# An attention's query blocks in another order, and three tiles fewer a head

## The chip, the cores and the metric

One core of a Trainium2 chip runs the whole program. Its engines are TensorE (PE, the matrix products), VectorE (DVE), ScalarE (ACT), GpSimd (POOL) and SyncE (SP); each takes its instructions in the order in which they were written, and waits for others by semaphores. POOL and SP here mostly issue DMA transfers. The metric is the device time of one execution in microseconds (us); of several executions the median counts.

## The reference

Two layers over 1024 rows of 1024 features. The change lies in the attention of the first: eight heads, each with two components of width 64 and values of width 128. A row sees all columns up to the end of its chunk of 64.

```python
def one_block(args):                       # 128 query rows at a time
    s = jnp.einsum('bqhcd,bkhcd->bhcqk', qb, k).astype(jnp.float32)
    s = jnp.where(allowed[None, None, None], s, -jnp.inf)
    p = jax.nn.softmax(s, axis=-1)
    a = p[:, :, 0] - lam * p[:, :, 1]
    return jnp.einsum('bqhk,bkhe->bqhe', a.astype(v.dtype), v)
...
o = rmsnorm(o, subln_g, SUBLN_EPS) * (1.0 - lambda_init)
return o.reshape(B, S, H * ATTN_V_DIM) @ w_o
```

q and k are first turned by rotary factors (`rope`). Around it stand norms, the residual, an MLP, a recurrent layer and a second MLP, which the change doesn't touch.

## The kernel before

**Slots.** The attention runs as 64 slots, eight for each of eight heads. A slot's position in its head picks a block of 128 query rows by the table `ORDER`; block b has scores of (b+1)*128 columns, so block 0 is the shortest and block 7 the longest. All engines but SP run in the order in which the loop of `attention` writes their instructions. What a slot writes, in order:

- `scores` of its block: products on PE (L737, L738), each component as two products with operands that are split in a high and a low part and stacked (`qs`, `ks`); then on DVE a mask and a maximum (L748 and L749 for blocks 0 to 3, whose two components share one bank of PSUM; L757 and L758 for each component of the longer ones), and on ACT the first component's exponential (L741). There are two banks for scores.
- fill work on PE, first part: steps (L584, L585, L587) of the next head's q and k projections, later of the output projection. `FILL_PART` says how much of a head's fill each of the slot's three parts gets.
- `keys_first`: the transposes (L784) of the block of the slot before, and their copies into `aT` on ACT (L961); then the second exponential of the slot's own block.
- one step of the side queue (`run_aside`), and what is due of `later`.
- fill, second part; `weighted`, the products with the values (L794) of the block two slots back, with an eviction and a square on ACT (L795, L797); fill, third part.
- `combine` on DVE (L769, L771, L772) of the slot's own block, and another step of the side queue.

**The side queue** is first in, first out; each of its two calls in a slot hands out one step that is due. Its steps are: the rotary factors of the next head's q or k (L677, L678, L674), each behind the transfers that swap halves; the low part of the product (L688, `low`), after which POOL issues the stacking transfers (L697, L698; four for q, eight for k: component 0 and 1 of one stack, then of the other); the scaling of a half head's output by its norm (L803 in `subln`); the low part of a turned half (L823 in `parts`), after which SP stores it. The high part of a product (L685) runs on ACT as soon as L674 has been written.

**Tiles.** Nearly every tile of 4 KB a partition comes from one pool, T, with 46 places (`BUFS`); they are given out in turn, and whoever writes into a place waits for the last reader of what was there, transfers included.

**Halves.** A head's eight output blocks are gathered as two halves (blocks 0 to 3, 4 to 7) in tiles `o4`. A half is normed and turned (`subln`, `turn_out`: PE L813, ACT L819 and L820) some slots after its block 3 or 7 is weighted; with the order of before, block 7 stands at position 3 and block 3 at position 7.

Functions and tables with the lines of the profile:

Of the kernel before, what the change touches and what calls it, by code (L numbers as in the profile page):

```python
# [9 lines left out]
F32 = mybir.dt.float32  # L10
F32R = mybir.dt.float32r
# [4 lines left out]
P = 128  # L16
# [25 lines left out]
class Second:  # L42
# [19 lines left out]
    def load(self, s):  # L62
        if s < self.loaded or s >= len(self.slots):
            return
        self.loaded = s + 1
        kind, (i, j) = self.slots[s]
        last, wv, hid, get, t4 = self.last, self.wv, self.k.hid, self.nc.sync.dma_start, self.k.t4
        w, x = t4("w2", F32, (P, 2, CH), "R"), t4("h2", F32, (P, 2, CH), "W")
        side = None
        if kind == "P":  # L70
            get(out=w, in_=wv[:, 0, i : i + 2, 0])
        elif kind == "A":
            get(out=w, in_=wv[:, 0, i])
            side = t4("w3", F32, (P, CH))
            get(out=side, in_=wv[:, 1, i, 1])
        elif kind == "B":
            get(out=w[:, 0], in_=wv[:, 1, i, 1 if last else 0])
            side = t4("w3", F32, (P, 2, CH))
            if last:
                get(out=side[:, 0], in_=wv[:, 0, i, 1])  # L80
            else:
                get(out=side, in_=wv[:, 0, i])
        else:
            get(out=w, in_=wv[:, 1, i : i + 2, 0 if kind == "C" or last else 1])
        if kind in "AB":
            at = {"A": 1, "B": 3}[kind]
            get(out=x, in_=hid[i][:, at : at + 2])
        else:
            at = {"P": 0, "C": 5, "D": 6}[kind]
            for n, b in enumerate((i, j)):  # L90
                get(out=x[:, n], in_=hid[b][:, at])
        self.raws[s] = w, x, side
# [158 lines left out]
    def run(self):  # L251
# [11 lines left out]
        self.prepare(0)  # L263
        for s in range(N - TAIL_SLOTS):
            self.load(s + AHEAD)
# [12 lines left out]
            self.drain(budget[kind])  # L278
        tail = range(N - TAIL_SLOTS, N)
        for s in tail[1:]:  # L280
# [10 lines left out]
class Trunk:  # L291
# [389 lines left out]
    def parts_of(self, q, then):  # L681

        nc = self.nc
        h, l = self.t4("qkh", F32R), self.t4("qkl", F32R)
        nc.scalar.activation(out=h, in_=q, func=AF.Copy)  # L685

        def low():
            nc.vector.tensor_tensor(out=l, in0=q, in1=h.bitcast(F32), op=ALU.subtract)  # L688
            then(h, l)

        self.aside(RL, low)
# [137 lines left out]
    def later(self, us, fn):  # L829
# [5 lines left out]
        while us > 0:  # L835
            us -= 2.8 + 0.65 * ORDER[s % NT]
            s += 1
        self.tasks.setdefault(s, []).append(fn)

    def aside(self, us, fn):  # L840
# [5 lines left out]
        while us > 0:  # L846
            us -= 2.8 + 0.65 * ORDER[s % NT]
            s += 1
# [19 lines left out]
    def attention(self):  # L868

        nc = self.nc
        while self.held:
            self.held.pop(0)()
        self.queue = []
        o = [None] * H
        wo = self.ins["attn_w_o"][0]
        blocks = [(h, kind) for h in range(H) for kind in "qk"]  # L880

        def halves(h):
            parts = []
            for p in range(2):
                t = self.t4("o", F32R)
                nc.sync.dma_start(out=t.bitcast(F32), in_=self.oT[h][p])
                parts.append(t)
            return parts

        def ahead(steps, at, box, load):  # L890
            for n, step in enumerate(steps):
                if n == at:
                    box.append(load())
                yield step

        def fills():
            box = [self.w_proj(*blocks[2])]
            first = []
            for b in range(2, len(blocks)):
                load = (lambda: self.w_proj(*blocks[b + 1])) if b + 1 < len(blocks) else (lambda: self.w_out(wo, 0, 4, 0))  # L900
                if b in OLOAD:
                    first += [halves(h) for h in OLOAD[b]]
                yield from ahead(self.proj_steps(*blocks[b], box.pop(0), "G"), 5, box, load)
            self.x = []
            for m in range(NK):
                at = 3 if m % 2 == 1 and m < NK - 1 else -1
                wt = box[0] if m % 2 == 0 else box.pop(0)
                was = self.raw(self.xT[m * P : (m + 1) * P, :], (P, S))
                self.x.append(self.t4("x"))
                yield from ahead(self.out_block(first, wt, m, m % 2, False, None, "G"), at, box, lambda: self.w_out(wo, 0, 4, (m + 1) * P))  # L910
                y = self.x[m]
                self.aside(1, lambda y=y, was=was: nc.vector.tensor_tensor(out=y, in0=y, in1=was, op=ALU.add))

        fill = fills()
        done = 0

        def fill_to(n):
            nonlocal done
            while done < n:
                step = next(fill, None)  # L920
                if step is None:
                    break
                done += step

        rate = (FILL_TOTAL - FILL_LEAD - FILL_KEEP) / H
        self.slot, self.tasks = 0, {}
        fill_to(FILL_LEAD)
        work = {}
        LT, LW, LO = LAGS
        os = []  # L930
        s = -1
        with self.tc.manual_schedule(engines={EPE, EACT, EDVE, EPOOL}):
            while s + 1 < H * NT or work or self.tasks or self.queue:
                s += 1
                self.slot = s
                h, pos = divmod(s, NT)
                i = ORDER[pos]

                def run(part):
                    f = (sum(map(sum, FILL_PART[:pos])) + sum(FILL_PART[pos][:part])) / sum(map(sum, FILL_PART))  # L940
                    if h < H:
                        fill_to(FILL_LEAD + rate * (h + f))
                    else:
                        fill_to(FILL_TOTAL - FILL_KEEP + FILL_KEEP * (3 * pos + part) / (3 * LO))

                os += [halves(g) for g in LATE.get(s - (H - 1) * NT, ())]
                exp2 = None
                if h < H:
                    if pos == 0:
                        if h == H - 1:  # L950
                            o[h] = [self.t4("oh", F32R), self.t4("ol", F32R)]
                        o4 = [self.t4("o4", F32, (P, 4, P)) for _ in range(2)]
                        ss = [self.sm("oss", 4) for _ in range(2)]
                    p, sums, exp2 = self.scores(h, i)
                    work[s] = [h, i, p, sums, o4[i // 4], ss[i // 4]]
                run(1)
                if s - LT in work:
                    wk = work[s - LT]
                    wk[2], outs = self.keys_first(wk[1], wk[2])
                    for dst, src in outs:  # L960
                        nc.scalar.activation(out=dst, in_=src, func=AF.Copy)  # L961
                if exp2:
                    exp2()
                self.run_aside(ASIDE[0])
                for fn in self.tasks.pop(s, ()):
                    fn()
                assert s not in self.tasks
                run(2)
                if s - LW in work:
                    wk = work.pop(s - LW)  # L970
                    self.weighted(*wk)
                    if wk[1] % 4 == 3:
                        self.later(1, lambda wk=wk: self.subln(wk[4], wk[5], lambda: self.turn_out(wk[0], wk[1] // 4, wk[4], o[wk[0]])))
                run(3)
                if s in work:
                    wk = work[s]
                    wk[2], wk[3] = self.combine(wk[1], wk[2], wk[3])
                self.run_aside(ASIDE[1] if h < H else 4)
            for _ in fill:
                pass  # L980
            self.run_aside(len(self.queue))
            self.slot = None
        self.os = os + [halves(h) for h in range(4 + len(os), H - 1)] + [o[H - 1]]
        self.w_lo = None
# [478 lines left out]
RS, RL, RN, RT, R3 = (10, 2, 3, 2, 3)  # L1463
ASIDE = (1, 1)
LAGS = (1, 2, 4)
FILL_PART = [(1.24, 1.17, 0.33), (0.74, 1.39, 0.4), (0.52, 1.0, 0.14), (0.74, 1.26, 0.4), (0.74, 1.0, 0.56), (0.79, 0.94, 0.37), (0.89, 1.18, 0.4), (1.04, 1.23, 0.4)]
ORDER = (4, 5, 6, 7, 0, 1, 2, 3)
ROWS = ((slice(0, HD), slice(HD, P)), (slice(HD, P), slice(0, HD)))
EPE, EACT, EDVE, EPOOL, ESP = (getattr(mybir.EngineType, e) for e in ("PE", "Activation", "DVE", "Pool", "SP"))
FILL_TOTAL, FILL_LEAD, FILL_KEEP = (288, 30, 10)  # L1470
OLOAD = {13: (0,), 14: (1, 2), 15: (3,)}
ORDER_A = (0, 1, 4, 5, 2, 3, 6, 7)
LATE = {7: (4,)}
TAIL_SLOTS = 4
AHEAD = 4
BUFS = {"R": 4, "W": 4, "T": 46}
# [26 lines left out]
```

## Time and profile before

| what | value |
|---|---|
| median of 3 executions | 2273.68 us (2269.03 to 2278.88) |
| the profiled execution | 2282.74 us, its span 2280.9 us |
| mean granted clock of TensorE in it | 0.975 |
| busy share of the span | PE 94%, DVE 67%, ACT 47%, POOL 4% |
| attention (158 to 610 us of the span) | 452 us, PE busy 383.67 us, clock 0.94 |

Times in the trace are microseconds from the span's start. The granted clock is a share of full speed: the clock has two levels, 1.0 (2.4 GHz) and 0.5 (1.2 GHz), and a share between them is a mean over a stretch. A row `[2.64 <-DVE p L772]` says that the engine sat idle 2.64 us before the instruction, and what ended the wait last by the profile.

### The profile page before, as it was taken

Reading aid. Unit: us, or ns where it says so; the run is one execution under the profiler, and the core shown is the slowest. Engines: PE = TensorE matmul, PEld = TensorE weight load, DVE = VectorE, ACT = ScalarE, POOL = GpSimd, SP = SyncE. Lnnn points to the kernel's source line nnn. Section 1 sums busy time; section 2 is a strip of 40 time slices with the busy share of each in tenths; the row PEclk is TensorE's granted clock in tenths of the full one; section 3 lists DMA queues with packets and bytes.
Section 4 is the critical chain, followed back from the end, with each engine's and each line's share of the span. In section 5 each row is a group of like instructions: output and inputs, shape, how many; then the busy total and the mean of one; then the engine's idle time right before and its main releaser. Section 6 shows DMA issues by size and latency. Waiting matters only on the chain.

```text
span 2280.9 us, 26452 instructions
## 1 busy us (share of the span) xinstructions
PE 2143.6 (94%) x9794; PEld 1763.2 (77%) x9794; DVE 1526.2 (67%) x2065; ACT 1069.0 (47%) x1627; POOL 102.6 (4%) x171
## 2 busy tenths in 40 slices
PE   8998888887999999999999999988999999799997
PEld 7786777776788888878888787777788888688885
DVE  5426667655697777658778467775977776476665
ACT  5225555554564444444335356652644443353433
POOL 3111112111000000000000000000000000000000
PEclk9999999988999999999999999998999999899999
DMA  6534435634524444398556412234244444874734
GB/s 193 143 83 114 114 102 133 167 106 113 178 97 153 152 153 152 136 371 282 208 178 219 133 46 85 72 111 143 102 156 152 152 152 150 323 254 162 239 111 147
DMA packets 236227, 355.82 MB, mean 156 GB/s; under 512 B 16226, under 2 KB 133059, under 8 KB 236099
## 3 DMA queue, kind: packets, MB, share of 16 engines
q1 hardware_dynamic: 227266, 326.87, 42.9%
q0 software_dynamic: 7680, 25.17, 4.8%
q10 hardware_dynamic: 1152, 2.10, 0.3%
q8 instruction: 77, 1.26, 0.2%
q14 instruction: 52, 0.42, 0.1%
HBM read 229.29 MB, written 91.23 MB: 141 GB/s over the span
## 4 chain that ended last, share of the span: by engine, by line
PE 62%; DVE 11%; ACT 10%; DMA 5%; issue 4%; POOL 1%; SPq 0%; ACTq 0%; POOLq 0%; DVEq 0%
PE acc L1192 5%; PE acc L1193 5%; PE acc L1194 5%; PE acc L145 4%; PE acc L143 4%; PE acc L144 4%; PE acg L1192 2%; PE acg L1194 2%; PE acg L1193 2%; ACT p L741 2%; PE acg L584 2%; PE acg L585 2%; PE acg L587 2%; PE acc L584 2%; PE acb L144 2%
## 5 line engine op out<-in xcount | busy, mean ns | idle before, releaser
L341 DVE TENSOR_TENSOR h2l<-h,h2h 128x1024 fp32r<-128x1024 f32 x112 | 136.7, 1221 | 72.5 <-ACT h2h L338 68.8
L1095 ACT ACTIVATE ct<-ct 128x1024 f32<-128x1024 f32 x64 | 67.9, 1061 | 250.3 <-DVE ct L1164 249.3
L741 ACT ACTIVATE p<-acc,nmax 128x768 f32<-128x768 f32 (+7 forms) x128 | 95.4, 745 | 153.3 <-DVE nmax L758 56.9
L338 ACT ACTIVATE h2h<-h 128x1024 fp32r<-128x1024 f32 x112 | 117.5, 1049 | 59.4 <-DMA h<-hid 51.4
L584 PE MATMUL acg<-xgh,wh 128*128 128x512 f32 x320 | 135.7, 424 | 0.0
L587 PE MATMUL acg<-xgh,wl 128*128 128x512 f32 x320 | 127.9, 400 | 0.0
L585 PE MATMUL acg<-xgl,wh 128*128 128x512 f32 x320 | 127.7, 399 | 0.0
L338 ACT ACTIVATE w2h<-w 128x1024 fp32r<-128x1024 f32 x80 | 84.2, 1053 | 86.1 <-DVE w L56 70.5
L143 PE MATMUL acc<-w2h,h2h 128*128 128x512 f32 x256 | 102.9, 402 | 7.2 <-ACT w2h L338 5.6
L144 PE MATMUL acc<-w2l,h2h 128*128 128x512 f32 x256 | 102.6, 401 | 5.4 <-DVE w2l L341 5.4
L414 POOL TENSOR_TENSOR rstd<-ms,mhalf 128x4 f32<-128x4 f32 (+2 forms) x25 | 25.0, 1002 | 1798.5 <-DVE ms L412 1777.9
L143 PE MATMUL acc<-h2h,w2h 128*128 128x512 f32 x256 | 101.1, 395 | 4.4 <-ACT w2h L338 4.2
L145 PE MATMUL acc<-h2h,w2l 128*128 128x512 f32 x256 | 101.5, 396 | 3.6 <-DVE w2l L341 3.6
L1164 DVE TENSOR_TENSOR cl<-cl,acc 128x512 f32<-128x512 f32 x64 | 60.9, 951 | 64.6 <-PE acc L1194 64.6
L341 DVE TENSOR_TENSOR w2l<-w,w2h 128x1024 fp32r<-128x1024 f32 x80 | 97.8, 1222 | 8.9 <-PE acc L144 4.9
L1192 PE MATMUL acc<-t12h,w12h 128*128 128x512 f32 x256 | 100.5, 393 | 2.4 <-DVE ct L1164 2.4
L145 PE MATMUL acc<-w2h,h2l 128*128 128x512 f32 x256 | 102.1, 399 | 0.0
L144 PE MATMUL acc<-h2l,w2h 128*128 128x512 f32 x256 | 101.2, 395 | 0.4 <-DVE h2l L341 0.4
L1193 PE MATMUL acc<-t12l,w12h 128*128 128x512 f32 x256 | 100.3, 392 | 0.0
L1194 PE MATMUL acc<-t12h,w12l 128*128 128x512 f32 x256 | 100.2, 391 | 0.0
L794 PEld LDWEIGHTS acb<-v,aT 128*128 128x128 f32 x576 | 74.8, 198 | 28.9 <-ACT aT L961 23.9
L794 PE MATMUL acb<-v,aT 128*128 128x128 f32 x576 | 80.1, 286 | 13.2 <-ACT aT L961 12.5
(377 smaller groups left out, 6077.4 us busy)
## 6 DMA issues: line engine op xcount, KB each, us to landing
w<-in_mlp_w_dram SPq DMA_DIRECT2D x96, 512.0 KB, 4.9
raw<-in_mlp_w_dram SPq DMA_DIRECT2D x64, 512.0 KB, 4.5
h<-hid SPq DMA_DIRECT2D x64, 512.0 KB, 5.3
h<-hid SPq DMA_DIRECT2D x96, 256.0 KB, 5.3
w<-in_mlp_w_dram SPq DMA_DIRECT2D x80, 256.0 KB, 4.0
hid<-cl SPq DMA_DIRECT2D x64, 256.0 KB, 2.0
hid<-h SPq DMA_DIRECT2D x32, 512.0 KB, 2.6
hid<-h SPq DMA_DIRECT2D x64, 256.0 KB, 2.1
```

Source lines behind the costliest of these rows:

```text
L143: mm(bank[m], ah, bh, start=first, stop=False)
L144: mm(bank[m], ah, bl, start=False, stop=False)
L145: mm(bank[m], al, bh, start=False, stop=end)
L338: nc.scalar.activation(out=hi, in_=src, func=AF.Copy)
L341: (lo_eng or nc.vector).tensor_tensor(out=lo, in0=src, in1=hi.bitcast(F32), op=ALU.subtract)
L584: mm(ps[:, pc], a, xh[:, cs], start=(k == 0), stop=False)
L585: mm(ps[:, pc], a, xl[:, cs], start=False, stop=False)
L587: mm(ps[:, pc], b, xh[:, cs], start=False, stop=(k == n - 1))
L794: nc.tensor.matmul(ps[:, :P], aT[:, j * P : (j + 1) * P], v[j // 2][:, j % 2, e], start=(j == 0), stop=(j == i))
L1192: mm(bank, ah[:, k], bh, start=k == 0, stop=False)
L1193: mm(bank, ah[:, k], bl, start=False, stop=False)
L1194: mm(bank, al[:, k], bh, start=False, stop=k == 3)
```

## The change

It has four parts. `ORDER` becomes (7, 0, 6, 1, 5, 2, 4, 3); `FILL_PART` is permuted with it, so that each block keeps its three numbers. The low part of a product is written over the product itself rather than into a tile `qkl`. The two `o4` tiles of a head become the halves of one. And a half is normed after the block of it that comes last in `ORDER` (`LAST_OF`: block 4, at position 6, and block 3, at position 7), since with the new order blocks 3 and 7 no longer end both halves.

```diff
@@ parts_of
-        h, l = self.t4("qkh", F32R), self.t4("qkl", F32R)
+        h, l = self.t4("qkh", F32R), q.bitcast(F32R)
@@ attention
-                        o4 = [self.t4("o4", F32, (P, 4, P)) for _ in range(2)]
+                        both = self.t4("o4", F32, (P, 2, 4, P))
+                        o4 = [both[:, 0], both[:, 1]]
...
-                    if wk[1] % 4 == 3:
+                    if wk[1] in LAST_OF:
@@ tables
-FILL_PART = [(1.24, 1.17, 0.33), (0.74, 1.39, 0.4), (0.52, 1.0, 0.14), (0.74, 1.26, 0.4), (0.74, 1.0, 0.56), (0.79, 0.94, 0.37), (0.89, 1.18, 0.4), (1.04, 1.23, 0.4)]
-ORDER = (4, 5, 6, 7, 0, 1, 2, 3)
+FILL_PART = [(0.74, 1.26, 0.4), (0.74, 1.0, 0.56), (0.52, 1.0, 0.14), (0.79, 0.94, 0.37), (0.74, 1.39, 0.4), (0.89, 1.18, 0.4), (1.24, 1.17, 0.33), (1.04, 1.23, 0.4)]
+ORDER = (7, 0, 6, 1, 5, 2, 4, 3)
...
+LAST_OF = [max((i for i in ORDER if i // 4 == g), key=ORDER.index) for g in range(2)]
```

Behind the tables' change the instructions of a head stand in another order. Two places show it. In the listings a row is a line, an operation, what it writes and what it reads; a number behind a name is the tile's.

VectorE in head 2, where the low part of head 3's k is made (the tile k, its high part `qkh`). Before, at position 4 (block 0, 128 columns):

```order
L748 MEMSET acc_2527 64x2x64
L749 TENSOR_REDUCE nmax<-acc_2527 128x2
L803 TENSOR_TENSOR o_240_1744<-o_240_1744,rstd 128x512
L769 RECIPROCAL rsum<-sums 128x2
L771 SCALAR_TENSOR_TENSOR fac<-sums,rsum,neglam 128x1
L772 SCALAR_TENSOR_TENSOR p_2525<-p_2526,fac,p_2525 128x128
L688 TENSOR_TENSOR qkl_2494<-k_2073,qkh_2493 128x1024
```

After, at position 6 (block 4, 640 columns), from the step ahead of it:

```order
L823 TENSOR_TENSOR ohl_2508<-ot_2507,ohl_2508 128x512
L757 MEMSET acc_2612 64x64
L758 TENSOR_REDUCE nmax<-acc_2612 128x1
L757 MEMSET acc_2619 64x64
L758 TENSOR_REDUCE nmax<-acc_2619 128x1
L823 TENSOR_TENSOR ohl_2517<-ot_2516,ohl_2517 128x512
L341 TENSOR_TENSOR wl_2649<-raw_2646,wh_2648 128x1024
L769 RECIPROCAL rsum<-sums 128x2
L771 SCALAR_TENSOR_TENSOR fac<-sums,rsum,neglam 128x1
L772 SCALAR_TENSOR_TENSOR p_2610<-p_2611,fac,p_2610 128x640
L688 TENSOR_TENSOR k_2071<-k_2071,qkh_2575 128x1024
```

The low part moved by two positions, from behind the combine of block 0 to behind that of block 4; the two L823 of the head before stand ahead of it, and one position (block 3) is left behind it.

ScalarE in head 1, where tiles of T are written whose last readers are stacking transfers (waits on DMASW semaphores). Before, at position 6 (block 2), two positions behind the low part of k:

```order
L741 ACTIVATE p_313_2151,sums_2149<-acc_315_2153,nmax_2150 128x384 [waits DMASW5_49,DMASW2_49,DMASW7_49,DMASW0_49,DVE_49]
L338 ACTIVATE wh_317_2169<-raw_316_2167 128x1024
L961 ACTIVATE aT_319_2173<-acb_320_2174 128x256 [waits PE_49]
L741 ACTIVATE p_314_2152,sums_2149<-acc_315_2153,nmax_2150 128x384 [waits DMASW4_49,DMASW6_49,DMASW3_49,DMASW1_49]
L795 ACTIVATE o4_240_1744<-acb_321_2189,rsum_2079 128x128 [waits DMAHW4_49,PE_49]
```

After, at position 5 (block 2), one position behind it:

```order
L741 ACTIVATE p_289_2056,sums_2054<-acc_291_2058,nmax_2055 128x384 [waits DVE_49,PE_49]
L962 ACTIVATE aT_296_2077<-acb_297_2078 128x512 [waits DMASW5_49,DMASW2_49,DMASW7_49,DMASW0_49,PE_49]
L962 ACTIVATE aT_296_2077<-acb_298_2083 128x256 [waits PE_49]
L741 ACTIVATE p_290_2057,sums_2054<-acc_291_2058,nmax_2055 128x384 [waits DMASW4_49,DMASW6_49,DMASW3_49,DMASW1_49]
L819 ACTIVATE ot_300_2097<-acb_299_2092,g08_706 128x512 [waits PE_49]
```

The waits moved from the two exponentials of a slot to a copy and an exponential one slot nearer to the transfers. (L961 is L962 in the changed code.)

## Rows read from the trace of the kernel before

**Rows 1.** Busy us of each engine (instructions), PEclk, DMA share, GB/s, of the attention.

```profile
158.00:610.00 452.00, 383.67 (x2081) 318.51 (x2080) 289.98 (x509) 248.12 (x642) 62.39 (x100) 0.94 0.45 119
```

**Rows 2.** Waits of PE in the attention: us in total, times, longest.

```profile
PE acb L784 <- DVE p L772: 25.5, 8, 5.8
PE acb L794 <- ACT aT L961: 12.5, 20, 1.7
PE acc L737 <- DMA ks<-qkh: 8.1, 4, 3.8
...
PE acb L813 <- ACT aT L961: 6.0, 4, 1.6
PE acb L784 <- DVE acc L757: 5.7, 4, 2.1
```

**Rows 3.** Timeline of PE: start, duration, instruction, idle before it.

```profile
203.89 0.52 PE L784 MATMUL acb<-ident,p 128*128 128x128 f32 x3 [2.64 <-DVE p L772]
...
262.93 0.87 PE L784 MATMUL acb<-ident,p 128*128 128x128 f32 x3 [4.97 <-DVE p L772]
...
319.16 0.87 PE L784 MATMUL acb<-ident,p 128*128 128x128 f32 x3 [5.83 <-DVE p L772]
...
456.08 1.30 PE L784 MATMUL acb<-ident,p 128*128 128x128 f32 x5 [5.75 <-DVE p L772]
...
477.10 0.69 PE L784 MATMUL acb<-ident,p 128*128 128x128 f32 x2 [6.57 <-ACT ot L819]
```

**Rows 4.** Timeline of ACT and DVE around two of those waits.

```profile
314.32 0.58 ACT L741 ACTIVATE p<-acc,nmax 128x384 f32<-128x384 f32 x1 [4.07 <-DMA ks<-qkl]
...
464.75 1.23 DVE L688 TENSOR_TENSOR qkl<-k,qkh 128x1024 fp32r<-128x1024 f32 x1
...
476.36 0.69 ACT L819 ACTIVATE ot<-acb,g 128x512 f32<-128x512 f32 x1 [10.27 <-DMA ks<-qkl]
```

**Rows 5.** The columns of rows 1 for two stretches behind long waits.

```profile
541.00:547.80 6.80, 4.98 (x13) 4.07 (x14) 2.47 (x5) 1.42 (x3) 0.00 (x0) 0.50 0.42 133
455.50:464.50 9.00, 8.41 (x40) 7.55 (x41) 5.17 (x11) 3.50 (x10) 0.00 (x0) 0.66 0.01 3
```

**Rows 6.** Groups of DVE in the attention: busy us, mean ns of one, idle before.

```profile
L341 DVE TENSOR_TENSOR wl<-raw,wh 128x1024 fp32r<-128x1024 f32 x11 | 13.5, 1226 | 31.8 <-ACT wh L338 31.8
...
L688 DVE TENSOR_TENSOR qkl<-k,qkh 128x1024 fp32r<-128x1024 f32 x7 | 8.5, 1218 | 0.0
...
L674 DVE TENSOR_TENSOR k<-k,sw 128x1024 f32<-128x1024 f32 x7 | 8.5, 1215 | 0.0
```

**Rows 7.** Timeline of PE and DVE where a slot of block 4 ends.

```profile
330.43 0.40 PE L737 MATMUL acc<-ks,qs 128*128 128x512 f32 x1
...
330.79 1.22 DVE L678 TENSOR_TENSOR sw<-sw,sin 128x1024 f32<-128x1024 f32 x1
```

**Rows 8.** Timeline of DVE and PE: k's low part, scores of heads 5, 7.

```profile
409.75 1.22 DVE L688 TENSOR_TENSOR qkl<-k,qkh 128x1024 fp32r<-128x1024 f32 x1
...
421.62 0.48 PE L737 MATMUL acc<-ks,qs 128*128 128x512 f32 x1
...
423.75 0.47 PE L737 MATMUL acc<-ks,qs 128*128 128x512 f32 x1 [1.26 <-DMA ks<-qkh]
...
529.94 1.22 DVE L688 TENSOR_TENSOR qkl<-k,qkh 128x1024 fp32r<-128x1024 f32 x1
...
541.08 0.76 PE L737 MATMUL acc<-ks,qs 128*128 128x512 f32 x1 [3.84 <-DMA ks<-qkh]
...
544.33 0.77 PE L737 MATMUL acc<-ks,qs 128*128 128x512 f32 x1 [1.74 <-DMA ks<-qkh]
```

**Rows 9.** Timeline of PE at the start of head 4's slot of block 3.

```profile
417.24 0.39 PE L737 MATMUL acc<-ks,qs 128*128 128x512 f32 x1
417.46 0.39 PE L738 MATMUL acc<-ks,qs 128*128 128x512 f32 x1
```

**Rows 10.** The transfers that L698 issues, over the whole span.

```profile
DMA to landing us min/median/max: 2.8/6.0/10.4
```

## The prediction

> **What bounds the kernel now.** I read the table by stretches first. In the attention stretch the tensor engine (PE) is busy 383.67 of 452 us at a mean granted clock of 0.94 [rows 1]; the diff moves nothing outside this stretch. So it offers 68.3 us of waits, and 452 x 0.06 = 27 us of low clock: at most 95 us. Next the waits of PE, which sort them in three. The largest group is transposes behind a combine (L784 <- L772), 25.5 us in 8 waits. A second is small waits between steps of the slots: L794 and L813 behind the copy L961 (12.5 and 6.0), L784 behind L757 (5.7), in all 24.2 us, none over 2.1. The third is scores (L737) behind stacking transfers, 8.1 us in 4 [rows 2].
>
> The timeline shows what the first group is. Five waits of 2.64, 4.97, 5.83, 5.75 and 6.57 us [rows 3] sum to 25.8 us, and the last of them leads on to ScalarE, whose L819 sat 10.27 us until a stacking transfer `ks<-qkl` had landed; ahead of the 5.83 us wait L741 sat 4.07 us for another [rows 4]. Neither reads such a transfer: each writes a tile of pool T that the transfer still reads. Behind the low part that ended at 464.75 + 1.23 = 465.98, L819 was free at 476.36, 10.4 us later [rows 4]. I take the other three to be of the same kind, judged by the same order of steps, and call all five **reuse waits**. After a long wait the clock is low for a while: granted 0.50 (1.2 of 2.4 GHz) in the 6.8 us behind the score waits of the last head (3.4 us lost) and 0.66 over 9 us around the 5.75 us wait (3.1 us lost) [rows 5]. I use 3.3 us for each long wait.
>
> **What the change takes away.** (a) A head takes 44 tiles from the ring of 46 (16 p, 8 aT, 14 for q and k, 2 o4, 4 for the turned output); three of them go, and every reuse comes later. I take all five reuse waits away: 25.8 + 5 x 3.3 = 42.3 us; bounds 21 (half of them come back elsewhere) and 42.3. (b) Long and short in turn: the step waits of the second group stand nearly all in slots of a long block behind another long one, where two long exponentials stand on ScalarE ahead of the copy L961. In the new order no long block (4 to 7) follows a long one. I keep 4 of the 24.2 us: -20; bounds 0 and -24.2.
>
> (c) The subtraction in place costs nothing: L674, which already writes over its own input in the same shape, takes 1215 ns, L688 1218 [rows 6]. The joint o4 tile adds no instruction.
>
> **What it adds.** (d) The listings show the fourth term. Both halves of a head now end at positions 6 and 7, so both L803 run at position 3 of the next head and both L823 at positions 5 and 6, in the queue that hands out two steps a slot, in the middle of the rotary and low-part chain of k. The low part of k for heads 3 to 6 moves from position 4 or 5 of the head before to the very last VectorE step of position 6. When does it end? In slots of block 4 the operation right behind the combine began at 330.79, while the next slot's scores began at 330.43 [rows 7]: at 0.4 us into the next slot, so it ends at 1.6. Ahead of the combine now also stand L823 and the weights' L341 of 1226 ns [rows 6], partly under the wait for the exponential: bounds 1.6 and 2.8, I take 2.0.
>
> From there the transfers. Eight are issued; component 0 needs the sixth, component 1 the eighth. Head 5: low part over at 409.75 + 1.22 = 410.97, scores of component 0 at 421.62 without a wait (10.65 later), of component 1 at 423.75 after a wait (12.8). Head 7: over at 531.16, component 0 at 541.08 after 3.84 us of waiting (9.9), component 1 at 544.33 (13.2) [rows 8]. I take 10.3 and 13.0. Only the slot of block 3 lies between: 421.62 - 417.24 = 4.4 us [rows 8, 9] as it stood, and 0.4 more, since it now transposes 5 tiles instead of 3 and weighs 3 instead of 2 (five transposes took 1.30 us in the stretch of low clock [rows 3], so about 0.13 each at the full one). So the next head's scores come 4.8 - 2.0 = 2.8 us behind the low part and wait 10.3 - 2.8 = 7.5; component 0's four products then take four steps of 0.22 (417.24 to 417.46) [rows 9], 0.9 us, and component 1 waits 13.0 - 10.3 - 0.9 = 1.8. With the clock 7.5 + 1.8 + 3.3 = 12.6, four times 50.4 us; before there are 1.3 us of this kind (423.75) [rows 8]: **+49.1**. With low ends of 1.6 and 2.8 it is 47.5 and 52.3.
>
> A rule of the Trainium skill speaks against this term. The median of the transfers of L698 from issue to landing is 6.0 us, the least 2.8 [rows 10]. The page "DMA: Bandwidth & Descriptors", section "Anatomy of one DMA — SWDGE (gpsimd) path", gives 2.0 us plus the bytes over 436e3 bytes a us, by which I estimate 2.6 us for the 256 KB of one. By it each stack would land 3.4 us sooner than that median, and the sum would come out some 33 us lower, at -28 instead of +6. The trace's median disagrees, its least value agrees.
>
> (e) The last head: its low part runs in position 7, behind the reduction, and ends some 3 us into the slot. Wait 10.3 - (4.8 - 3.0) = 8.5, then 1.8, with the clock 13.6; before 3.84 + 1.74 [rows 8] and 3.4 of clock [rows 5], 9.0: **+4.6**. (f) Head 1, position 5 (block 2): its copy and second exponential now write tiles that the stacks of the low part one slot earlier still read, where in before the same wait came two slots behind and gave the 4.97 us. One slot (some 5 us) less cover: 5 + 5 + 3.3 = **+13.3**; bounds 6 and 17. The first boundary, heads 0 to 1: +1.
>
> **Sum.** -42.3 - 20 + 49.1 + 4.6 + 13.3 + 1 = +5.7 us. The profiled execution took 2282.7 us, 0.4% over the median of 2273.7; on its own scale the sum gives 2288.4, on that of the median 2279.4: I say 2279. Unknown costs: (a) up to +21, (b) -4 to +20, (d) -2 to +2, (f) -7 to +4.
>
> **Rivals.**
> *Faster: the stalls are shorter.* Suppose that the last stacks land as quickly as behind the low part of 464.75, where ScalarE was let go after 10.4 us instead of 13 [rows 4], and the sixth as much sooner. Then each of the four stalls is 2.6 us less, the 4 us of step waits that I kept vanish beneath the stalls, and head 1 stands at its low end: 4 x 2.6 + 4 + 7 = 21 less, 2258. For it: while PE stalls, fewer weights are loaded beside the stacks. Against: 12.8 and 13.2 us in two heads of different load [rows 8]. Chance 0.22.
>
> *Faster: the transfers don't hold each other up.* If each of the eight lands in the least time of 2.8 us instead of the median of 6.0 [rows 10], all of them come 3.2 us sooner: 3.2 in each of six places (four heads, the last head, head 1) is 19, and if the clock then stays up in the four heads another 13: 32 less, 2247. The Trainium skill's page above states such a time for a single transfer. Since here they come in eights and the median is over twice the least, the chance is 0.06.
>
> *Slower: the short block gives no cover.* The transposes of a long block wait for its combine, and what hides that chain is the next slot's score products. Behind block 6 they were block 7's 4096 columns and are now block 1's 1024; behind block 5 they were block 6's 3584 and are now block 2's 1536; behind block 4 they were 3072 and are now 2048. That is 6144 columns a head less; at 0.22 us for 512 [rows 9] 2.6 us, in 8 heads 21 us. It decides where the chain of exponentials and combine ends later than PE's fill. Against it: block 7 is followed by block 0 in both orders, and none of the five long waits but one (456.08) stands there. It gives 2300; chance 0.18.
>
> *Slower: the reuse waits only move, and the change doesn't free what it is said to free.* The stacks are now issued at the end of a head, and the slots behind them reuse tiles as before: half of (a), 21 us, comes back. 2300; chance 0.12. The forecast has 0.42.
>
> **How the numbers follow.** A measurement of this kernel tells about 0.5%, 11 us, from no change, so "same" is 2262 to 2285. The forecast's own bounds, some -13 to +20 where not all of them go one way, put most of it there and some in either tail: faster 0.30 (the faster rivals and a little), same 0.38, slower 0.32. The range takes in the first rival and both slower ones: 2248 to 2302; outside lie most of the second rival and the far tails.
>
> **What would show it.** Right: PE's waits L737 <- DMA ks rise from 8.1 to 40 us or more, with stalls of 7 to 9 us ahead of heads 3 to 7; the waits L784 <- L772 fall below 5 us; the step waits below 6; ScalarE sits some 12 us at block 2 of head 1; PE's waits in all stay near 68 us and the clock near 0.94. Wrong: L737 <- DMA under 25 us (the transfers are quicker or the low part earlier), or L784 <- L772 still over 15 (cover lost, or reuse moved). The stretches behind the attention keep their lengths within 1 us; if not, the tiles' new places matter there and I have missed it.

## The result and the profile after

The changed kernel takes 2291.97 us (median of 4, 2289.68 to 2293.62), the kernel before 2274.84 us (4 runs): ratio 1.0077, 95% interval 1.0056 to 1.0099. It is 17 us slower. The forecast was 2279, its range 2248 to 2302.

The attention of the profiled execution, and the waits of PE in it. The first row is one of a view by stretches (PE, PEld, DVE, ACT, POOL busy us, granted clock, DMA share, GB/s), to be held against [rows 1]; the others are PE's waits (us in total, times, longest), against [rows 2].

```profile
158.00:627.00 469.00, 383.97 (x2100) 318.18 (x2099) 291.45 (x510) 251.36 (x644) 59.89 (x100) 0.93 0.44 117
```

```profile
PE acc L737 <- DMA ks<-qkh: 32.3, 7, 8.1
PE acb L794 <- ACT aT L962: 21.3, 21, 2.7
PE acb L813 <- ACT aT L962: 20.1, 7, 9.9
PE acb L784 <- DVE p L772: 8.7, 10, 1.6
...
PE acb L784 <- DVE acc L757: 0.7, 1, 0.7
```

PE is busy for as long as before (383.97 against 383.67 us). The two stretches are rough ones; the exact cuts follow below. The scores' wait for stacks rose from 8.1 to 32.3 us; the transposes' wait for the combine fell from 25.5 to 8.7, with no single one over 1.6. But two of the three kinds of small waits that were to shrink (L794 and L813 behind the copy) grew from 18.5 to 41.4 us; 14.7 of these are two long ones, below. The third (L784 behind L757) fell from 5.7 to 0.7.

To see where the 17 us lie I cut both profiled executions at the first scores of the first slot and of the last. Between them lie 436.4 us before and 448.3 after. By the records of PE, its waits (over 50 ns) take 66.2 and 83.4 us; low clock while PE was busy costs 21.4 and 17.9; the rest, its work at full clock, is 348.8 and 347.0. So **waits +17.2, clock -3.4, work -1.9**. Ahead of the attention 2.3 us were added, behind it some 3.6 taken off, as the two rows of the stretches behind show (before, then after); the two executions differ by 10.6 us in all. The medians differ by 17, since the profiled execution of before lay 7.9 us over its median, that of after 1.4.

```profile
595.00:2281.00 1686.00, 1626.84 (x7135) 1335.40 (x7133) 1183.28 (x1431) 774.16 (x891) 7.76 (x11) 0.98 0.49 167
```

```profile
609.20:2291.60 1682.40, 1625.15 (x7143) 1334.02 (x7141) 1183.54 (x1433) 774.27 (x890) 8.05 (x11) 0.99 0.49 167
```

The timeline of PE after shows the long waits (start, duration, instruction, idle ahead of it and what ended it):

```profile
250.67 1.11 PE L813 MATMUL acb<-ident,o 128*128 128x128 f32 x4 [9.86 <-ACT aT L962]
...
321.95 0.77 PE L737 MATMUL acc<-ks,qs 128*128 128x512 f32 x1 [4.55 <-DMA ks<-qkh]
...
377.94 0.76 PE L737 MATMUL acc<-ks,qs 128*128 128x512 f32 x1 [4.06 <-DMA ks<-qkh]
...
435.22 0.77 PE L737 MATMUL acc<-ks,qs 128*128 128x512 f32 x1 [7.02 <-DMA ks<-qkh]
...
469.03 0.69 PE L813 MATMUL acb<-ident,o 128*128 128x128 f32 x2 [4.84 <-ACT aT L962]
...
500.61 0.76 PE L737 MATMUL acc<-ks,qs 128*128 128x512 f32 x1 [6.28 <-DMA ks<-qkh]
...
562.37 0.76 PE L737 MATMUL acc<-ks,qs 128*128 128x512 f32 x1 [8.05 <-DMA ks<-qkh]
```

Five of the seven stand ahead of the first scores of heads 3 to 7, where the prediction had put them. The one at 250.67 is block 2 of head 1: ScalarE's copy waited for the stacks of k (7.94 us), and the turn of a half (L813) for that copy.

```profile
250.02 0.87 ACT L962 ACTIVATE aT<-acb 128x512 f32<-128x512 f32 x2 [7.94 <-DMA ks<-k]
```

One of the five boundaries in full, head 2 to 3. VectorE first, then PE and ScalarE: block 3's scores begin at 309.72; L341 sat 1.74 us ahead of the combine until ScalarE had its high part; the low part of k ends at 313.13, 3.4 us into the slot; the copy that L794 needs is late by 2.21 us, since on ScalarE it stood behind block 3's first exponential, which had waited 3.86 us for the maximum, and mask and maximum stood behind the combine and the low part on VectorE; the next head's scores start at 321.95, 8.8 us behind the low part.

```profile
309.51 1.23 DVE L341 TENSOR_TENSOR wl<-raw,wh 128x1024 fp32r<-128x1024 f32 x1 [1.74 <-ACT wh L338]
...
311.91 1.22 DVE L688 TENSOR_TENSOR k<-k,qkh 128x1024 fp32r<-128x1024 f32 x1
```

```profile
309.72 0.48 PE L737 MATMUL acc<-ks,qs 128*128 128x512 f32 x1
...
316.47 0.71 PE L794 MATMUL acb<-v,aT 128*128 128x128 f32 x4 [2.21 <-ACT aT L962]
```

```profile
314.66 0.69 ACT L741 ACTIVATE p<-acc,nmax 128x512 f32<-128x512 f32 x1 [3.86 <-DVE nmax L749]
```

### The profile page after: what moved, and what is told of

Same layout as the page of the kernel before. It is cut to its first block, busy times and chain, and to the rows that moved or that the text cites. A ratio compares the mean times of both kernels' runs of the same rounds, so it can differ in the third digit from the quotient of the medians.

```text
span 2291.6 us, 26453 instructions
## 1 busy us (share of the span) xinstructions
PE 2137.5 (93%) x9794; PEld 1757.3 (77%) x9794; DVE 1525.7 (67%) x2065; ACT 1070.5 (47%) x1627; POOL 100.1 (4%) x171
## 4 chain that ended last, share of the span: by engine, by line
PE 66%; DVE 12%; ACT 9%; DMA 6%; issue 5%; POOL 1%; SPq 0%; ACTq 0%; POOLq 0%; DVEq 0%
PE acc L1193 5%; PE acc L1194 5%; PE acc L1195 5%; PE acc L145 4%; PE acc L143 4%; PE acc L144 4%; PE acg L1193 2%; PE acg L1195 2%; PE acg L1194 2%; PE acg L584 2%; PE acg L585 2%; PE acg L587 2%; PE acc L584 2%; PE acc L585 2%; PE acc L587 2%
## 5 line engine op out<-in xcount | busy, mean ns | idle before, releaser
L341 DVE TENSOR_TENSOR h2l<-h,h2h 128x1024 fp32r<-128x1024 f32 x112 | 136.7, 1221 | 72.0 <-ACT h2h L338 68.3
L741 ACT ACTIVATE p<-acc,nmax 128x128 f32<-128x128 f32 (+7 forms) x128 | 95.3, 744 | 162.1 <-DVE nmax L758 71.1
L737 PE MATMUL acc<-ks,qs 128*128 128x512 f32 (+2 forms) x192 | 72.7, 386 | 34.1 <-DMA ks<-qkh 32.3
L341 DVE TENSOR_TENSOR w2l<-w,w2h 128x1024 fp32r<-128x1024 f32 x80 | 97.8, 1222 | 8.9 <-PE acc L144 4.9
L794 PEld LDWEIGHTS acb<-v,aT 128*128 128x128 f32 x576 | 72.3, 192 | 35.2 <-ACT aT L962 31.9
```

Source lines behind the costliest of these rows:

```text
L341: (lo_eng or nc.vector).tensor_tensor(out=lo, in0=src, in1=hi.bitcast(F32), op=ALU.subtract)
L741: nc.scalar.activation(out=p[c][:, :n], in_=src, func=AF.Exp, bias=nmax[:, c : c + 1], accum_out=sums[:, c : c + 1])
```

## Experiments

Each kernel was timed beside the kernel before; the ratios are to it, with 95% intervals. The changed kernel stands at 1.0077. They ran on three chips, so that ratios compare better than medians. The order of blocks with all of the old tiles (`order_only`) gave no result: with the two separate `o4` tiles and the separate `qkl` its instructions would wait for one another in a circle (a deadlock), so there is no such kernel to time. With the joint `o4` and a separate `qkl`, as in `order_o4`, it runs.

| run | what it is | median us | ratio |
|---|---|---|---|
| tiles_only | old order, the tiles of the change | 2276.63 | 1.0011 (0.9998 to 1.0024) |
| order_o4 | new order, low part in its own tile | 2290.15 | 1.0060 (1.0045 to 1.0075) |
| late_k | old order, low part of k later | 2299.45 | 1.0105 (1.0087 to 1.0123) |
| early_low | changed kernel, low part of k sooner | 2281.45 | 1.0026 (1.0013 to 1.0038) |
| chain_first | changed kernel, k's chain first in the side queue | 2283.30 | 1.0040 (1.0026 to 1.0054) |
| relief_early | early_low, ten tiles a head fewer | 2274.74 | 1.0002 (0.9993 to 1.0011) |
| sp_stack | changed kernel, half the stacks on SP | 2285.76 | 1.0048 (1.0034 to 1.0063) |
| before_sp | kernel before, half the stacks on SP | 2264.34 | 0.9961 (0.9946 to 0.9975) |
| before_allsp | kernel before, all stacks on SP | 2270.78 | 0.9980 (0.9969 to 0.9991) |
| relief_early_sp | relief_early, half the stacks on SP | 2268.98 | 0.9978 (0.9968 to 0.9987) |
| early_sp | early_low, half the stacks on SP | 2285.41 | 1.0045 (1.0027 to 1.0064) |
| tiles_sp | tiles_only, half the stacks on SP | 2270.94 | 0.9981 (0.9968 to 0.9994) |

### Do fewer tiles take the reuse waits away?

`tiles_only` is the kernel before with the two tile edits of the change and nothing else:

```diff
-        h, l = self.t4("qkh", F32R), self.t4("qkl", F32R)
+        h, l = self.t4("qkh", F32R), q.bitcast(F32R)
...
-                        o4 = [self.t4("o4", F32, (P, 4, P)) for _ in range(2)]
+                        both = self.t4("o4", F32, (P, 2, 4, P))
+                        o4 = [both[:, 0], both[:, 1]]
```

> The old order of blocks with the low part in place and the joint o4 tile. Theory of the prediction (the three tiles remove the reuse waits): 20 to 42 us faster than before, 2233 to 2255, and the five waits of 2.6 to 6.6 us are gone. Rival (the place in the order decides, since the ring turns with the same step whether it has a few tiles more or less): the waits of heads 1, 2 and 5 stay, within 6 of before, 2268 to 2277.

No change that can be told. Of the five reuse waits [rows 3] the first, the smallest, is gone, and the score waits grew by about as much (8.1 to 11.3 us in all); the other four stand at the same blocks, one as a wait of L794:

```profile
262.70 0.52 PE L784 MATMUL acb<-ident,p 128*128 128x128 f32 x3 [3.91 <-DVE p L772]
...
318.41 0.44 PE L784 MATMUL acb<-ident,p 128*128 128x128 f32 x1 [5.57 <-DVE p L772]
...
452.50 0.58 PE L794 MATMUL acb<-v,aT 128*128 128x128 f32 x1 [9.06 <-ACT aT L962]
...
476.43 0.47 PE L784 MATMUL acb<-ident,p 128*128 128x128 f32 x1 [6.20 <-ACT ot L819]
```

The rival holds: here the count doesn't decide. `order_o4` asks the same in the new order, with one of the edits undone:

```diff
-        h, l = self.t4("qkh", F32R), q.bitcast(F32R)
+        h, l = self.t4("qkh", F32R), self.t4("qkl", F32R)
```

> The changed kernel with the low part of a product in a tile of its own again; the order of blocks, the joint o4 tile and the half-head rule stay. If the order alone decides which tile waits for which transfer (as tiles_only says), the waits stand in the same places as in the changed kernel: 9 to 10 us at block 2 of head 1, 30 to 35 us of L737 behind stacks, within 6 of it, 2286 to 2298. If the place saved by writing over the product removes reuse waits in this order, they come back here: 2300 or more.

Again no difference beside the changed kernel (2290.15 against 2291.97), and nearly the same waits, as the two views of PE's waits show (above, and here):

```profile
PE acc L737 <- DMA ks<-qkh: 33.1, 9, 6.9
PE acb L794 <- ACT aT L962: 21.4, 21, 2.7
PE acb L813 <- ACT aT L962: 20.2, 7, 10.0
PE acb L784 <- DVE p L772: 8.8, 10, 1.6
```

So the order of blocks, with the half-head rule that goes with it, moved the reuse waits, and writing the low part in place did nothing for them. The tile addresses of the programs before and tiles_only fit that: in both a place of the pool is given out again most often 9 tiles later, less than two slots, where a ring of 46 places would give 46. I had taken the pool for a ring of fixed step, and its places for given out in turn; they are not.

### Does the late low part of k cost what the sum said?

`late_k` leaves everything of the kernel before and only makes the low part due later:

```diff
-RS, RL, RN, RT, R3 = (10, 2, 3, 2, 3)
+RS, RL, RN, RT, R3 = (10, 5, 3, 2, 3)
```

> The kernel before, its order of blocks unchanged, with the low parts due later (5 us behind L674 instead of 2): k's low part moves from position 5 to position 6 in heads 3 to 5 and the scores of heads 4 to 6 have some 4 to 5 us less until their stacks land; heads 2 and 3 keep theirs. Theory (late stacks cost what the prediction's sum says): L737 waits for stacks of 2 to 6 us ahead of each of heads 4 to 6, each with up to 3.4 us of clock, in all +12 to +25; against it the wait of 10.3 us of ScalarE at block 2 of head 5 goes (its tile was read by stacks one slot earlier), some -9: 2278 to 2291. If late stacks are covered by other work: 2265 to 2274.

It is 1.05% slower, 23 us, 8 us beyond the upper end of that theory. PE's score waits in all, then two of them with a reuse wait between:

```profile
PE acc L737 <- DMA ks<-qkh: 34.2, 7, 9.8
```

```profile
441.01 0.77 PE L737 MATMUL acc<-ks,qs 128*128 128x512 f32 x1 [9.85 <-DMA ks<-qkh]
...
474.64 0.58 PE L794 MATMUL acb<-v,aT 128*128 128x128 f32 x1 [7.37 <-ACT aT L961]
...
506.37 0.77 PE L737 MATMUL acc<-ks,qs 128*128 128x512 f32 x1 [7.74 <-DMA ks<-qkh]
```

Score waits rise from 8.1 to 34.2 us, in the old order and with the old tiles: a low part one position later is enough. Not all stand where the expectation put them: 6.05 us lie ahead of head 1. The reuse wait at block 2 of head 5 went, as expected, while the one ahead of it grew from 5.75 to 7.37 us.

`early_low` goes the other way in the changed kernel: k's chain of steps takes precedence in the side queue, and the low part is due at once.

```diff
...
-        self.aside(RL, low)
+        self.aside(RL, low, 0)
...
-        for at, fn in list(self.queue):
+        for item in sorted(self.queue, key=lambda q: q[2]):
+            at, fn = item[:2]
...
-RS, RL, RN, RT, R3 = (10, 2, 3, 2, 3)
+RS, RL, RN, RT, R3 = (10, 0, 3, 2, 3)
```

> The changed kernel with the rotary and low-part steps ahead of the others in the side queue, and the low part due at once: k's low part ends one slot sooner, behind the combine of block 2 at position 5. Theory (the late stacks are the loss): PE's waits L737 <- DMA fall from 32.3 us to under 8, the clock lost behind them (some 20 us in heads 3 to 7) mostly returns, 35 to 50 us faster than the changed kernel, 2242 to 2257. Rival (short blocks give no cover): waits behind L772 and L962 take their place, a gain under 15, over 2277.

The score waits went, the time hardly followed: 10.5 us (0.5%) faster than the changed kernel by the medians, where 35 to 50 us were expected. That is the rival's gain of under 15 us, but the longest of the waits that came are of another kind. PE's waits, then three waits of ScalarE:

```profile
PE acb L784 <- DVE p L772: 24.3, 14, 11.1
PE acb L794 <- ACT aT L963: 20.3, 20, 2.1
PE acc L737 <- ACT p L741: 17.1, 4, 10.3
...
PE acc L737 <- DMA ks<-qkh: 2.8, 3, 1.0
```

```profile
ACT p L741 <- DMA ks<-k: 11.6, 1, 11.6
ACT aT L963 <- issue: 9.5, 2, 8.4
ACT p L741 <- DMA olT<-ohl: 8.7, 1, 8.7
```

The score waits fell from 32.3 to 2.8 us. In their place ScalarE waits for tiles that transfers still read: k's stacks, and the stores of a turned half (`olT<-ohl`), whose low part L823 was pushed back in the queue. These cost PE 10.26, 11.07 and 4.85 us. What the 8.4 us at the copy waited for the trace doesn't name.

`chain_first` has the precedence without the earlier due time (RL stays 2), so that the low part is the first step of position 6 instead of its last.

> The changed kernel with the rotary and low-part steps ahead of the others in the side queue, at unchanged due times: k's low part stays at position 6 but is the first of that slot's two steps instead of the last, ahead of the combine, some 4 us sooner. Theory (the late stacks are the loss): L737 <- DMA falls from 32.3 us by 4 us in each of four or five heads, to 12 to 18, and the time by 12 to 22 to 2270 to 2280. Rival (the waits are handed on to the reused tiles, as in early_low): under 8 us faster, 2284 or more.

Faster than the changed kernel by 0.4%, in the middle between the two. L737 still waits 27.1 us for stacks:

```profile
PE acc L737 <- DMA ks<-qkh: 27.1, 8, 5.7
```

Ahead of head 3 the low part is made sooner (at 303.37 rather than 311.91), but POOL's stacks themselves now waited for the store, and the scores came 13.9 us behind the low part rather than 8.8. The row of POOL and that of PE:

```profile
306.48 0.57 POOL L697 DMA_DIRECT2D ks<-qkh  x1 [23.42 <-DMA olT<-ohl]
```

```profile
318.53 0.77 PE L737 MATMUL acc<-ks,qs 128*128 128x512 f32 x1 [5.39 <-DMA ks<-qkh]
```

`relief_early` takes ten tiles a head out of early_low: the transposed block is copied over the dead second p, and the turned half's low part over its product.

```diff
-        aT = self.t4("aT")
...
-                    wk[2], outs = self.keys_first(wk[1], wk[2])
+                    wk[2], outs = self.keys_first(wk[1], wk[2], self.others.pop(s - LT))
...
-            t, both = self.t4("ot", F32, (P, CH)), self.t4("ohl", F32R, (P, 2, CH))
+            both = self.t4("ohl", F32R, (P, 2, CH))
+            t = both[:, 1, :].bitcast(F32)
```

> early_low with ten tiles a head fewer: the transposed block is copied over the dead second-component tile p instead of a tile aT, and the turned half's low part is written over its product in one tile. If the count of tiles sets the reuse waits, those of early_low (8.7 us of ScalarE behind a store olT<-ohl at block 4 of head 2, 11.1 us of PE at block 3 of head 3, 11.6 us of ScalarE behind ks<-k at block 4 of head 5) go, and it is 20 to 35 us faster than early_low, 2246 to 2261. If the pool hands out whatever place was given back last, so that a transfer's source is rewritten soon however many tiles there are, the waits only move: within 8 of early_low, 2273 to 2289.

It is 6.7 us faster than early_low by the medians (0.24% by the ratios), within the rival's 8, and level with the kernel before. ScalarE's waits for transfers have moved rather than gone:

```profile
ACT p L741 <- DMA ks<-k: 11.3, 1, 11.3
ACT p L741 <- DMA olT<-ohl: 9.8, 1, 9.8
ACT p L741 <- DMA qs<-q: 4.7, 1, 4.7
```

### What spaces the landings?

`sp_stack` and `before_sp` move the second transfer of each stack from POOL's queue to SP's, in the changed kernel and in the kernel before; `before_allsp` moves both.

```diff
-        self.nc.gpsimd.dma_start(out=t.bitcast(F32)[b], in_=second.bitcast(F32)[a])
+        self.nc.sync.dma_start(out=t.bitcast(F32)[b], in_=second.bitcast(F32)[a])
```

> The changed kernel with the second transfer of each stack issued by SP's queue instead of POOL's. If the eight transfers hold each other up because they share one queue, they land up to 4 us sooner, L737 <- DMA falls from 32.3 to between 10 and 18 us, and the time by 15 to 25 to about 2270. If they share the DMA engines, or if SP stands behind other loads, the landings stay or get later: L737 <- DMA 30 or more, time 2287 or more.

> The kernel before with the second transfer of each stack on SP's queue. If the reuse waits end with the landing of the stacks (theory), they shorten by 2 to 4 us each where a stack of k is waited for (heads 1, 2 and 5, and the score waits of heads 5 and 7): 8 to 16 us faster than before, 2259 to 2267. If something else sets them, within 4 of before, 2271 to 2279.

> The kernel before with all transfers of the stacks on SP's queue, none on POOL's. If POOL's queue is what spaces the landings by some 1.1 us, they land sooner still than with half of them on SP: another 3 to 8 us faster than before_sp, 2256 to 2262. If the spacing is that of any single queue: about as before, 2270 to 2280.

Half on SP is worth 6 us in the changed kernel and 10 in the kernel before; all on SP less (5 us). The first of these misses its theory (15 to 25 us), the second is inside it, the third takes the side of the rival. In sp_stack the waits of scores that the profile puts down to the stacks fell from 32.3 to 14.9 us, as expected, but others of L737 came, with no cause named or behind other transfers:

```profile
PE acc L737 <- DMA ks<-k: 9.0, 2, 4.8
PE acc L737 <- DMA ks<-qkh: 5.9, 2, 5.0
PE acc L737 <- issue: 5.6, 2, 3.3
```

All waits of L737 fell from 34.1 to 25.2 us, and PE's waits in all between the two cuts from 83.4 to 74.0; low clock beside its work rose from 17.9 to 23.8, so that most of this was lost again in the profiled execution. In before_sp it went the other way: waits 66.2 to 61.7, low clock 21.4 to 11.2.

The queue doesn't set the pace at which the bytes move. Stretches of 10 us in which the stacks of head 6's k land, from before and from before_sp, move as much: 210 and 203 GB/s, with a DMA share of 0.89 and 0.88.

```profile
466.00:476.00 10.00, 4.53 (x29) 3.79 (x27) 1.99 (x5) 0.09 (x1) 3.77 (x8) 0.96 0.89 210
```

```profile
461.00:471.00 10.00, 3.47 (x20) 2.73 (x18) 1.12 (x2) 0.11 (x1) 1.01 (x2) 0.85 0.88 203
```

Eight transfers of 256 KB are 2.1 MB, and 10 us at 210 GB/s are 2.1 MB: in these stretches the DMA engines are nearly full, whoever issues the transfers. An earlier issue can be part of the gain; how much of it was not tried apart. SP isn't bound to the loop's order, and in sp_stack it issued a transfer of the high part at 310.34, ahead of the low part at 312.21, so that one transfer less was left:

```profile
310.34 0.50 SPq L698 DMA_DIRECT2D ks<-qkh  x1
```

```profile
312.21 1.22 DVE L688 TENSOR_TENSOR k<-k,qkh 128x1024 fp32r<-128x1024 f32 x1
```

> The kernel relief_early with the second transfer of each stack on SP's queue, as in sp_stack. Transfers that land sooner end both the score waits and the reuse waits sooner: 5 to 15 us faster than relief_early. If SP's own loads and stores behind them come later instead, 0 to 10 slower.

2268.98 against 2274.74: 6 us, as expected.

### Is long and short in turn worth anything once its costs are off?

> The changed kernel with k's low part one slot sooner (as early_low) and the second transfer of each stack on SP's queue (as sp_stack): the new order of blocks without its two known costs. If long and short in turn is worth something by itself, it beats before_sp (2264): 2245 to 2260. If the short blocks give no cover (waits behind L772 and L962 of some 40 us stay, as in early_low) the order brings nothing: 2264 to 2280.

> tiles_only with the second transfer of each stack on SP's queue: the old order of blocks with the same tiles and queues as early_sp. If the tiles bring nothing by themselves, as tiles_only says, it is within 6 of before_sp: 2258 to 2270. If fewer tiles help once the stacks land sooner: 2250 to 2257.

`early_sp` and `tiles_sp` have the same tiles and the same queues; the first has the new order with k's chain early, the second the old order. 2285.41 against 2270.94: the new order with that early chain loses 14 us, is slower than both of its expectations, and isn't better than early_low (the intervals overlap). tiles_sp lies 0.9 us outside its 6. But the costs of early_sp are not off, as its expectation had it: its largest waits, 22.2 us of the scores for ScalarE (L737 <- L741), are handed on as in early_low, since ScalarE's exponentials sat 29.0 us until transfers had landed. So the 14 us don't price the order alone. The waits behind the combine and the copy stay too:

```profile
PE acc L737 <- ACT p L741: 22.2, 5, 11.6
PE acb L794 <- ACT aT L963: 20.1, 21, 2.1
PE acb L784 <- DVE p L772: 17.5, 15, 2.9
PE acb L813 <- ACT aT L963: 15.3, 7, 5.2
```

In all kernels with either order L794 waits for the copy some 20 times. My reading, not tried apart: a block of more than four tiles takes both of its PSUM banks for its transposes, and the products with the values need one back; there are four such blocks a head in any order. The places of the waits fit it: 19 of the 20 of before and all 21 of the changed kernel stand in slots that transpose one of the blocks 4 to 7. In the changed kernel these slots' own blocks are all short. The best kernel of the study is `before_sp`, 0.39% faster than before (2264.34 us), with the old order.

## Why the prediction came out as it did

The sign of the sum and the place of the largest loss were right, its size too small by 5 us on the profiled executions and by 11 on the medians. That the sum came so near is in part luck: (b) was 24 us too favourable, (d) and (e) together 17 us too unfavourable. The terms, as forecast and as the two profiles have them (waits of PE, and low clock while it is busy):

| step | forecast | measured | how |
|---|---|---|---|
| (a) reuse waits of before go | -42.3 | -39.0 | 25.8 of waits and 13.3 of clock; all five gone |
| (b) waits between steps | -20 | +4.0 | 32.4 before, 36.4 after: all waits less reuse and score waits |
| (c) in place, joint tile | 0 | about 0 | tiles_only 1.0011, order_o4 level with the changed kernel |
| (d) score waits, heads 3 to 6 | +49.1 | +34.2 | 24.2 of waits, less 1.3; clock 2.8 each |
| (e) last head | +4.6 | +2.3 | 8.05 for 5.6; clock 3.6 for 3.7 |
| (f) block 2 of head 1 | +13.3 | +11.4 | 9.86 and 1.5 of clock |
| first boundary | +1 | -1.2 | a wait of before went |
| block 5 of head 5 | none | +6.4 | 4.84 and 1.5 of clock: a reuse wait not forecast |

Less 4.4 us of clock that before lost elsewhere and 1.9 us of work this makes the 11.9 us between the two cuts.

**The step that failed is (b).** I took the small waits as set by two long exponentials ahead of the copy, and cut them from 24.2 to 4 us. Without the two long ones they are 27.4 (L794 21.3, L813 5.4, L784 behind L757 0.7): only the last of the three went. In the changed kernel all of the L794 waits stand in slots whose own block is short, so two long exponentials can't be what made them. They go with the slot that transposes a long block, whichever block is its neighbour; why is only argued above. The largest three (2.2, 2.2 and 2.7 at the ends of heads 2, 3 and 5) stand where the late low part is ahead of the next block's mask, but it made at most a part of them: early_low, whose low part is a slot sooner, keeps 1.7 and 2.1 at heads 2 and 5.

**In (d) the mechanism was right and its parts were off.** Landing of the sixth transfer ran from 8.5 to 11.6 us behind the low part where I had used 10.3; the low part ended 1.3 to 4.1 us into the slot rather than 2.0, at head 2 at 3.4, since L341 waited for ScalarE (my bound of 2.8 left that out). The clock cost less than 3.3 a stall. late_k shows the mechanism by itself.

**In (a) the amount was right and the reason wrong,** so that its amount is luck too. I gave the credit to three tiles fewer; tiles_only and order_o4 show that the order moved the waits. With it falls my listing of the bounds: the half that could "come back elsewhere" was not a matter of the count, and it did come back in part, at blocks 2 of head 1 and 5 of head 5, and wholesale in early_low.

**The rivals.** "The short block gives no cover" is there in small: transposes behind a combine take 8.7 us in ten waits of up to 1.6, where before had 6.4 beside its reuse waits: some 2 more, not 21. The page of the Trainium skill that was weighed in (d) ("DMA: Bandwidth & Descriptors", section "Anatomy of one DMA — SWDGE (gpsimd) path") gives a single transfer its time; the landings of eight together, 8.5 us or more for the sixth, speak against its use here.

**Of the profile's marks** score waits (32.3 for "40 or more") and combine waits (8.7 for "below 5") moved the way named and stopped short, and so did ScalarE's wait at block 2 of head 1 (7.94 for "some 12"); the step waits ("below 6", measured 27.4) did not; PE's waits rose by 17 us and did not "stay near 68"; the stretches behind the attention differ by 3.6 us instead of 1, with the busy times alike. Such a difference comes without the change too: from the first scores of the last slot to the end, late_k, with the order and the tiles of before, takes 1680.6 us and before 1686.2.

**What stays open:** what the order is worth by itself; why early_sp gains nothing on early_low from its stacks on two queues; whether before_sp and tiles_sp differ (6.6 us by the medians, but their intervals overlap); why the profiled execution of before_sp lost less to low clock and that of sp_stack more; and what exactly the copy of early_low waited for at block 3 of head 3.

## What to carry to other kernels

When a table reorders blocks, follow the side work: find the one step that the next stage waits for (here the low part of k and its eight transfers), and see how many slots are left behind it in the new order. A stall that was taken away by moving work earlier came back here as a wait for the tile that the moved work still holds; counting tiles didn't tell where. And before waiting transfers are blamed on a queue, put their bytes beside the DMA share of the stretch.

## What the runs showed of the hardware that I had not expected

The clock can fall while PE is still waiting, and that part of the low stretch is free. In the 9.86 us wait at head 1, in which PE ran nothing, the granted clock was 0.63 on average: 3.6 us of the loss lay there, and only 1.5 us (6.8 us at 0.78) in the work behind it. The two stretches, during and behind the wait:

```profile
240.90:250.60 9.70, 0.00 (x0) 0.00 (x0) 0.41 (x1) 1.26 (x4) 2.44 (x5) 0.63 0.97 239
250.70:257.50 6.80, 6.80 (x30) 5.81 (x31) 2.48 (x7) 3.32 (x9) 0.00 (x0) 0.78 0.29 81
```

A longer wait thus need not be followed by a larger loss of clock: around the 5.75 us wait of before 3.1 us were lost [rows 5]. The same first row shows the DMA engines at 0.97 and 239 GB/s while PE and, for most of it, ScalarE wait for the eight transfers of k's stacks, about 1.1 us for each 256 KB.
